# A decoder step's feed-forward down product: two of three token slices computed as seven rounds of half products

## The chip, the core and the metric

The kernel runs as one program on one core of a Trainium2 chip. The metric is the device time of one execution in microseconds (us). The engines named here: PE (TensorE, the matrix engine; PEld is its weight load), DVE (VectorE), ACT (ScalarE), POOL (GpSimd) and SP (SyncE, which only issues transfers). Each engine works through its own queue in order and waits for others by semaphores. Matrix products read SBUF and write PSUM; large arrays lie in HBM and move by DMA.

## What is computed

One step of a two-layer decoder (an mLSTM layer, then a forgetting-attention layer) for a prompt of 1024 tokens with 16 meta tokens and for 8 x 8 sample tokens, together 1104 tokens, model width 1024. Each layer ends with a feed-forward part, and that is what matters here:

```python
D_FF = -(-8 * D_MODEL // (3 * 256)) * 256          # 2816

def swiglu(xn, w_gu, w_d):
    gu = xn @ w_gu
    return (jax.nn.silu(gu[..., :D_FF]) * gu[..., D_FF:]) @ w_d
...
        h = h + swiglu(rmsnorm(h, prm['norm_ffn'][l]), prm['w_gate_up'][l], prm['w_down'][l])
```

The last product, the hidden activations (1104 x 2816) by `w_down` (2816 x 1024), is called the down product.

## The kernel before

All products are made in pairs of rounded float32 (`fp32r`): an operand is split into a high part (cast on ACT) and a rest (subtraction on DVE; `split`, L330 to L332), and a product is three matmuls, high by high, high by rest, rest by high (`mm3`, L267 to L271). The tokens are cut into three slices of 368 (`SL`, t = 0, 1, 2). Activations stand with their features on the 128 partitions, so a hidden vector is 22 blocks of 128 rows (`NF`).

`ffn` (L1465) runs once a layer, with three parts.

*Gate/up* (L1654 to L1805). The gate and up products of hidden blocks 2 to 21 already work on combinations of slices and weights: a `Unit` makes 20 products of 6 matmuls for two blocks of rows and three slices, even units the gate, odd units the up side; DVE and ACT combine the PSUM banks into six results (`s1`, `c15`, `s2`, `e`, `t4`, `v2`, each 128x368). `out` (L1530) applies silu to an even unit's results and multiplies an odd unit's with them; the products are the hidden activations, stored to HBM (`hT`) by SP, six stores every second unit. POOL makes the weight sums that a unit needs (`PairWeights.sums`, L102 to L111), two units ahead, from weights that SP loads (L77). The first two blocks of rows are made directly (`direct`, L1654).

*The down loop* (L1821 to L1856). `seq` lists 66 units (t, z, c): slice t, half z of the 1024 outputs, c one of 11 pairs of hidden blocks. A unit takes one weight block of 256 x 512 and one activation block of 256 x 368 and makes 4 groups of 6 matmuls, one for each of 4 PSUM banks; 11 units accumulate, and at the last unit of such a run DVE adds each bank to the residual `H[t]` (L1834; the addition is L1491). Two units ahead of their use, `w_split` and `h_split` split the raw blocks; weights are loaded by SP (`w_load`, L1638) into three raw buffers (two slots and `wr`), activations by POOL (`h_load`, L1621) into three buffers (`hr`). Activations of a slice are loaded and split in its half z = 0 and kept for z = 1. Split weights rotate through four places, so a split waits until PE has left the unit four back.

*Beside the loop.* After a bank is added, `each` squares the row block on ACT and sums the squares on POOL (`add_sq`, L393 to L405). When a slice is done, `ends` starts a generator of which one step runs in each unit: in layer 0 the normalisation of the slice (`norm_x`, L407 to L441; storing it to HBM first, L616), in layer 1 the final normalisation, transposes and stores (`final`, L1873). The residuals are reloaded from HBM during the loop (L1851, at units 2, 16 and 38 in the program).

Order: inside the loop the orders of PE, DVE and ACT are those of the program (`manual_schedule`); POOL and SP are ordered by the planner that builds the kernel, which goes by when its own model finds an instruction ready, with the program's order as priority.

## Time and profile before

| what | value |
|---|---|
| time, median of 3 runs | 2844.2 us (2840.56 to 2845.89) |
| the profiled execution's own time | 2841.83 us |
| span of its trace | 2840.1 us |
| granted TensorE clock, mean | 0.996 |
| HBM read, written | 299.5 MB, 96.8 MB |
| POOL's activation loads for the loop (L1621), all | 60 of 368 KB, and 8 more into the slices' own space |
| SP's weight loads for the loop | 88 into the two slots, 42 into `wr`, 2 into other space |

The down loops of layer 0 and layer 1 stand at 998.9 to about 1267 us and about 2557 to 2829 us. In a row of a table by stretch, each engine's busy us are followed by its instructions in brackets. In a row of groups, after the bar: busy us of the group, mean ns of one instruction, idle us of the engine just before, and what ended that idle time. A timeline row gives the start, the length, engine, line, operation, tiles, and in brackets the idle time before it. A tile's name is followed by others where buffers are shared: `vA` (layer 0) and `Ht` (layer 1) hold residuals, raw weights and intermediate results.

### The profile page before, as it was taken

The numbers are of one execution on the slowest core, as the hardware profiler recorded it, in microseconds if no ns is written. First come the engines' busy times: TensorE is split into PE (matmuls) and PEld (weight loads), VectorE is DVE, ScalarE is ACT, GpSimd is POOL, SyncE is SP. The second block draws the span as 40 slices with busy tenths as digits, with TensorE's granted clock in tenths as the row PEclk, the third lists the DMA queues.
The fourth block names the chain that finished last, engine by engine and source line by source line (L and its number), as shares of the span: only waits on it lengthen the run. The fifth ranks groups of instructions, "written<-read, shape, count | busy, mean of one in ns | idle before, by whom it ended". The sixth has DMA issues, their size and how long they took to land. (4 is left out here: it accounts for less than half of the span.)

```text
span 2840.1 us, 54146 instructions
## 1 busy us (share of the span) xinstructions
PE 2773.6 (98%) x20630; PEld 2651.7 (93%) x20630; DVE 1743.6 (61%) x3606; ACT 1318.1 (46%) x2636; POOL 1085.0 (38%) x1582
## 2 busy tenths in 40 slices
PE   8999998999999999999999999999999999999999
PEld 7997988999999999999999888777999999999998
DVE  6144566687787755553466543777478777775553
ACT  6122464444444434443345444877344454443432
POOL 3042333066656411117572202555307666631210
PEclk9999999999999999999999999999999999999999
DMA  7156664122222275644453676442413222236653
GB/s 218 29 139 166 164 182 156 53 89 77 82 85 79 94 267 194 207 156 142 132 174 120 238 289 221 135 171 88 159 50 91 78 78 90 77 109 243 214 191 106
DMA packets 313974, 399.81 MB, mean 141 GB/s; under 512 B 28966, under 2 KB 235794, under 8 KB 312690
## 3 DMA queue, kind: packets, MB, share of 16 engines
q1 hardware_dynamic: 277282, 277.66, 30.8%
q0 software_dynamic: 35680, 118.12, 12.9%
q8 instruction: 162, 2.65, 0.4%
q14 instruction: 98, 0.80, 0.1%
q10 hardware_dynamic: 752, 0.57, 0.1%
HBM read 299.50 MB, written 96.77 MB: 140 GB/s over the span
## 5 line engine op out<-in xcount | busy, mean ns | idle before, releaser
L332 DVE TENSOR_TENSOR slot<-slot,slot 128x1024 fp32r<-128x1024 f32 (+3 forms) x263 | 252.6, 962 | 117.2 <-ACT slot L331 111.8
L331 ACT CAST slot<-slot 128x1024 fp32r<-128x1024 f32 (+3 forms) x263 | 206.5, 787 | 227.9 <-PE dps L270 95.9
L1515 PE MATMUL m<-x0h,slot 128*128 128x368 f32 x640 | 178.3, 329 | 0.0
L1515 PE MATMUL m<-x1h,slot 128*128 128x368 f32 x640 | 174.1, 331 | 2.7 <-DVE ns L1492 0.9
L1621 POOL DMA_DIRECT2D hr<-hT x60 | 32.5, 541 | 271.9 <-DVE T_2l L332 68.1
L111 POOL TENSOR_TENSOR slot<-vA 128x256 f32<-128x256 f32 x80 | 75.4, 952 | 149.8 <-DMA vA<-in_w_gate_up 77.6
L111 POOL TENSOR_TENSOR slot<-Ht 128x256 f32<-128x256 f32 x80 | 75.1, 949 | 150.3 <-DMA Ht<-in_w_gate_up 78.6
L1515 PE MATMUL m<-x2h,slot 128*128 128x368 f32 x480 | 132.3, 330 | 0.0
L332 DVE TENSOR_TENSOR slot<-Ht,slot 128x256 fp32r<-128x256 f32 (+3 forms) x101 | 88.1, 874 | 56.3 <-ACT slot L331 56.3
L332 DVE TENSOR_TENSOR slot<-vA,slot 128x256 fp32r<-128x256 f32 (+3 forms) x101 | 88.1, 874 | 55.4 <-ACT slot L331 55.4
L1515 PEld LDWEIGHTS m<-x1h,slot 128*128 128x128 f32 x640 | 115.6, 188 | 4.6 <-DVE vA L1491 1.5
L1515 PEld LDWEIGHTS m<-x0h,slot 128*128 128x128 f32 x640 | 116.1, 188 | 0.0
L405 POOL TENSOR_TENSOR ns<-ns,nq 128x368 f32<-128x368 f32 x50 | 56.6, 1133 | 142.5 <-ACT nq L403 136.5
L1515 PE MATMUL m<-x1l,slot 128*128 128x368 f32 x320 | 105.6, 330 | 0.0
L1515 PE MATMUL m<-x0l,slot 128*128 128x368 f32 x320 | 105.5, 330 | 0.0
L2641 ACT ACTIVATE s<-s,nb 128x272 f32<-128x272 f32 (+7 forms) x126 | 98.8, 786 | 0.0
L2676 ACT COPY th<-tp 128x768 f32<-128x768 f32 (+1 forms) x80 | 73.6, 921 | 47.4 <-PE tp L2668 25.8
L1515 PE MATMUL m<-T_2h,slot 128*128 128x368 f32 x320 | 93.8, 334 | 0.4 <-ACT vA L1521 0.4
L1515 PE MATMUL m<-T_4h,slot 128*128 128x368 f32 x320 | 93.7, 334 | 0.0
L326 DVE SCALAR_TENSOR_TENSOR slot<-slot,gain,slot 128x256 fp32r<-128x256 f32 (+2 forms) x152 | 63.7, 466 | 43.5 <-ACT slot L325 41.1
L332 DVE TENSOR_TENSOR slot<-wr,slot 128x1024 fp32r<-128x1024 f32 x42 | 53.5, 1274 | 60.0 <-ACT slot L331 60.0
L1515 PEld LDWEIGHTS m<-x2h,slot 128*128 128x128 f32 x480 | 86.9, 188 | 0.0
(867 smaller groups left out, 10362.3 us busy)
## 6 DMA issues: line engine op xcount, KB each, us to landing
slot<-in_w_down SPq DMA_DIRECT2D x88, 512.0 KB, 4.6
hr<-hT POOLq DMA_DIRECT2D x60, 368.0 KB, 5.4
wr<-in_w_down SPq DMA_DIRECT2D x42, 512.0 KB, 3.8
wraw<-in_w_in_a SPq DMA_DIRECT2D x40, 512.0 KB, 4.2
vA<-in_w_gate_up SPq DMA_DIRECT2D x40, 512.0 KB, 4.1
Ht<-in_w_gate_up SPq DMA_DIRECT2D x40, 512.0 KB, 4.2
kp<-in_cache_k SPq DMA_DIRECT2D x32, 512.0 KB, 5.9
vp<-in_cache_v SPq DMA_DIRECT2D x32, 512.0 KB, 8.4
```

Source lines behind the costliest of these rows:

```text
L111: self.net.nc.gpsimd.tensor_tensor(out=o, in0=a, in1=b, op=op)
L326: nc.vector.scalar_tensor_tensor(out=lo[:, k], in0=raw[:, k], scalar=gk, in1=hi[:, k].bitcast(F32), op0=ALU.mult, op1=ALU.subtract)
L331: self.nc.scalar.copy(hi, src)
L332: self.nc.vector.tensor_tensor(out=lo, in0=src, in1=hi.bitcast(F32), op=ALU.subtract)
L405: (nc.vector if x >= late else nc.gpsimd).tensor_tensor(out=s, in0=s, in1=sq, op=ALU.add)
L1515: nc.tensor.matmul(u.b[b][:, :SL], w[p][:, k], x[q][:, k], start=new and k == i == 0, stop=k == 1 and i == 2, skip_group_check=True)
L1621: nc.gpsimd.dma_start(hraw[j], hT[t][:, 2 * c : 2 * c + 2])
L2641: nc.scalar.activation(ss[z, u], ss[z, u], AF.Exp, bias=nb[:, z : z + 1], accum_out=sm[:, u, z : z + 1])
L2676: nc.scalar.copy(th.rearrange("p x z (u h q) -> p h (x z u) q", h=2, q=64)[:, :, :n], pt[:, :, :n])
```

## The change

For hidden blocks 2 to 21, the down products of slices 1 and 2 are no longer made as four sets of products (two slices, two output halves) but as seven. Slices 1 and 2 with the even and odd hidden blocks are a 2 x 2 matrix of activations A11, A12 (slice 1, even and odd) and A21, A22 (slice 2); the weights with even and odd hidden blocks and the two output halves are a 2 x 2 matrix too. `ROUNDS` lists the seven products in their order, each as (number, weight block to load, which results it is added to, with sign): 5 (A11 + A12), 1 (A11 + A22), 3 (A11), 7 (A12 - A22), 4 (A22), 2 (A21 + A22), 6 (A21 - A11). Each round is 5 units of 256 hidden rows.

- The loop has 61 units: 22 for slice 0 as before, 4 for the first pair of hidden blocks (slices 1 and 2, both halves, each a run of its own), 35 for the rounds.
- The five sums of activations are made in gate/up by POOL (`combine`), once an odd unit, from its results, over the buffers of those results; five sums and the two plain blocks that rounds 3 and 4 need go to HBM (`hA`), with slice 0's two: nine stores every second unit.
- Of the weights, two of the four blocks are loaded once and kept (the odd block of half 1 in round 5, in the space of slice 1's activations; the even block of half 0 in round 1, in the space of gate/up's `T` tiles). Rounds 5 and 2 use a kept block as it is. Rounds 1, 3, 7, 4 and 6 need a sum or difference of two blocks, made on POOL (`w_sum`, 128x1024) before the split: round 1 from both kept blocks, the others from a newly loaded and a kept one.
- Every round's activations are loaded and split: 48 loads a layer in place of 34; weight blocks are split 59 times in place of 66, loaded 54 times in place of 66.
- A round's banks are added to up to two results (12 additions of four tiles over the seven rounds, and 4 more for the first pair of hidden blocks, in place of 4 in all).
- Slice 1 is done after round 4 and slice 2 after round 6; in the last two rounds two steps of the generator run a unit, and three of the pending squares. The splits stand ahead of a unit's matmuls in the program, behind them before.
- The residuals' reload stands at units 2, 14 and 18, and the final output's buffers are others.

```diff
+ROUNDS = ((5, None, ((1, 1, 1), (1, 0, -1))), (1, None, ((1, 0, 1), (2, 1, 1))), (3, (0, 1), ((1, 1, 1), (2, 1, 1))),
+          (7, (1, 0), ((1, 0, 1),)), (4, (1, 0), ((1, 0, 1), (2, 0, 1))), (2, None, ((2, 0, 1), (2, 1, -1))),
+          (6, (0, 1), ((2, 1, 1),)))
...
-    hT = [self.dram.tile([P, NF, SL], F32, name=f"hT{l}_{t}") for t in range(3)]
+    hT = [self.dram.tile([P, NF if t == 0 else 2, SL], F32, name=f"hT{l}_{t}") for t in range(3)]
+    hA = {r: self.dram.tile([P, NF // 2 - 1, SL], F32, name=f"hA{l}_{r}") for r in range(1, 8)}
...
                     tt(out=o, in0=o, in1=keep[t, i], op=ALU.mult)
-                    nc.sync.dma_start(hT[t][:, u.f + i], o)
+                    if t == 0:
+                        nc.sync.dma_start(hT[0][:, u.f + i], o)
+                    elif (t, i) in ((1, 0), (2, 1)):
+                        u.send(3 if t == 1 else 4, c)
                 else:
                     nc.scalar.activation(o, o, AF.Silu)
                     keep[t, i] = o
+
+            def send(u, r, c):
+                nc.sync.dma_start(hA[r][:, u.f // 2 - 1], u.c[c])
+
+            def combine(u):
+
+                pool = lambda o, i, j, op: nc.gpsimd.tensor_tensor(out=u.c[o], in0=u.c[i], in1=u.c[j], op=op)
+                for r, o, i, j, op in ((7, "v2", "s1", "t4", ALU.subtract), (5, "s1", "s1", "s2", ALU.add),
+                                       (1, "c15", "s2", "t4", ALU.add), (2, "t4", "t4", "e", ALU.add),
+                                       (6, "e", "e", "s2", ALU.subtract)):
+                    pool(o, i, j, op)
+                    u.send(r, o)
...
-        seq = [(t, z, c) for t in range(3) for z in range(2)
-               for c in ((*range(1, NC), 0) if (t, z) == (2, 1) else range(NC))]
-
-        hseq = [i for i, (t, z, c) in enumerate(seq) if z == 0 or (t, c) == (2, 0)]
-        hraw, hpart, wraw, wpart = {}, {}, {}, {}
+        NR = (NC - 1) // 2
+        ws = [("p", 0, c, z) for z in range(2) for c in range(NC)] + [("p", 1, 0, z) for z in range(2)]
+        ws += [("r", x, q, None) for x in range(len(ROUNDS)) for q in range(NR)]
+        hs = [(0, c) for c in range(NC)] + [(1, 0), (2, 0)] + [("r", x, q) for x in range(len(ROUNDS)) for q in range(NR)]
+
+        seq = [(j, j % NC, 0, j // NC, j % NC == 0, j % NC == NC - 1) for j in range(2 * NC)]
+        seq += [(2 * NC + z, NC + t - 1, t, z, True, True) for z in range(2) for t in (1, 2)]
+        seq += [(2 * NC + 2 + i, NC + 2 + i, None, i // NR, i % NR == 0, i % NR == NR - 1) for i in range(len(ROUNDS) * NR)]
+        wneed, hneed = ([max(e[k] for e in seq[: i + 1]) for i in range(len(seq))] for k in (0, 1))
+        flow = [j for j, w in enumerate(ws) if w[0] == "p" or ROUNDS[w[1]][0] not in (5, 2)]
...
+                if hs[j][0] == "r":
+                    _, x, q = hs[j]
+                    src = hA[ROUNDS[x][0]][:, 2 * q : 2 * q + 2]
...
+                y = (x0 + x1 + a)[j] if j < NC else x2[(j - NC) % 4]
+                hpart[j] = tuple(p[:, : 2 * SL].rearrange("p (k n) -> p k n", k=2) for p in y)
+                self.split(hraw.pop(j), *hpart[j])
...
+        halves = wd.rearrange("(c h p) n -> p h c n", h=2, p=P)
+
+        def own(h, q):
+
+            if h:
+                if q % 3 == 0:
+                    kept["x", q // 3] = self.xp.tile([P, KT * SLA], F32, name=self.uid("wx"), tag="x1" + "hl"[q // 3])
+                return view(kept["x", q // 3][:, q % 3 * KT * P : q % 3 * KT * P + KT * P])
+            return view(fp.tile([P, 4 * SL], F32, name=self.uid("wt"), tag="T%d%s" % ((2, 1, 4)[q // 2], "hl"[q % 2])))
...
+                if i in flow:
+                    k = flow.index(i)
+                    if k < 3:
+                        wraw[i] = view((self.slots[0], self.slots[1], flat[1])[k])
+                    else:
+                        wraw[i] = view((self.slots[0], self.slots[1], wr)[(k if kind == "p" else k + 2) % 3])
+                if kind == "p":
+                    nc.sync.dma_start(wraw[i], wd[2 * q * P : 2 * q * P + 2 * P, 512 * z : 512 * z + 512].rearrange(
+                        "(k p) n -> p k n", p=P))
+                    return
+                r, b, _ = ROUNDS[x]
+                part = lambda h, z: halves[:, h, 1 + 2 * q : 3 + 2 * q, 512 * z : 512 * z + 512]
+                if r in (5, 1):
+                    h = 1 if r == 5 else 0
+                    kept[h, q] = own(h, q)
+                    nc.sync.dma_start(kept[h, q], part(h, h))
+                if r in (5, 2):
+                    wraw[i] = kept[1 if r == 5 else 0, q]
+                if b:
+                    nc.sync.dma_start(wraw[i], part(*b))
+
+        def w_sum(i):
+            if i < len(ws) and ws[i][0] == "r":
+                _, x, q, _ = ws[i]
+                r, b, _ = ROUNDS[x]
+                if i in flow:
+                    nc.gpsimd.tensor_tensor(out=wraw[i], in0=wraw[i] if b else kept[0, q],
+                                            in1=kept[0 if r in (4, 6) else 1, q], op=ALU.subtract if r in (3, 4) else ALU.add)
 
         def w_split(i):
-            if i < len(seq):
-                wpart[i] = tuple(view(self.slots[y]) for y in (2 + i % 4, LOW[i % 4]))
+            if i < len(ws):
+                p = (i + max(0, min(3, (i - 2 * NC + 3) // 5))) % 4
...
+                    if g == 2 and v.odd:
+                        v.combine()
...
+            u.combine()
...
+            for i, (wi, hi, t, z, lead, last) in enumerate(seq):
+                n = SL
+                k, todo = min(i + 2, len(seq) - 1), None
+                while wj < wneed[k]:
+                    wj += 1
+                    w_split(wj)
+                    todo = wj
+                while hj < hneed[k]:
+                    hj += 1
+                    h_split(hj)
+                    h_load(hj + 3)
+                if todo:
+                    w_sum(todo + 1)
+                if len(seq) - 4 < i < len(seq) - 1 and after:
+                    early(i - len(seq) + 3)
+                wh, wl = wpart[wi]
+                ah, al = hpart[hi]
+                to = ((t, z, 1),) if t is not None else ROUNDS[z][2]
...
-                        add(H[t][:, 4 * z + m], H[t][:, 4 * z + m], o)
-                        pend.append(lambda t=t, m=4 * z + m: each(t, m))
+                        for tt_, zz, sign in to:
+                            y = H[tt_][:, 4 * zz + m]
+                            (add if sign > 0 else sub)(y, y, o)
+                        if (t == 0 or (t is None and ROUNDS[z][0] in (3, 4, 2, 6))):
+                            tq, zq = (0, z) if t == 0 else {3: (1, 1), 4: (1, 0), 2: (2, 0), 6: (2, 1)}[ROUNDS[z][0]]
+                            done.append(tq)
+                            x = done.count(tq) - 1
+                            pend.append(lambda t=tq, m=4 * zq + m, x=x: each(t, m, x))
+                            if x == KT - 1 and tq < 2:
+                                pend.append(lambda t=tq: ends(t))
...
-                if last and z and t < 2:
-                    pend.append(lambda t=t: ends(t))
-                w_split(i + 2)
...
-                if i + 2 in hseq:
-                    h_split(hj)
-                    h_load(hj + 3)
-                    hj += 1
-                w_load(i + 5)
-                if i in (2, 16, 38):
-                    y = (2, 16, 38).index(i)
+                if todo:
+                    w_load(todo + 3)
+                if i in (2, 14, 18):
+                    y = (2, 14, 18).index(i)
                     nc.gpsimd.dma_start(H[y], self.hD[:, :, TS[y][0] : TS[y][1]])
-                next(steps, None)
+                late = t is None and z > 4
+                for _ in range(0 if late and last else 2 if late else 1):
+                    next(steps, None)
                 if not last:
-                    for _ in range(2):
+                    for _ in range(3 if late else 2):
                         if pend:
                             pend.pop(0)()
+            for _ in steps:
...
-    out = flat[(2, 0, 1)[t]]
+    out = flat[t - 1] if t else self.xp.tile([P, KT * SLA], F32, name="outs", tag="x0h")
```

47 lines of the change are left out of this document (19 added, 28 removed).

## The prediction

> **What bounds the kernel now.** I read the page's first lines, then the table of busy time by stretch (laid over the down loop), then the groups by line with shapes kept apart, then timelines of single engines.
>
> ```profile
> span 2840.1 us, 54146 instructions
> PE 2773.6 (98%) x20630; PEld 2651.7 (93%) x20630; DVE 1743.6 (61%) x3606; ACT 1318.1 (46%) x2636; POOL 1085.0 (38%) x1582
> ```
>
> TensorE is the bound of nearly the whole span, so the question is whether the down loop is one of its saturated stages. Its six stretches of layer 0, then one of layer 1 (us; busy us and instructions of PE, PEld, DVE, ACT, POOL; clock, DMA share, GB/s):
>
> ```profile
> 998.90:1043.00 44.10, 44.10 (x264) 44.10 (x263) 22.99 (x25) 16.63 (x20) 8.35 (x13) 1.00 0.90 320
> 1043.00:1087.40 44.40, 44.40 (x267) 44.40 (x266) 17.78 (x17) 15.57 (x19) 5.65 (x8) 1.00 0.43 139
> 1087.40:1131.70 44.30, 44.30 (x264) 44.06 (x263) 29.52 (x36) 20.13 (x26) 7.56 (x13) 1.00 0.74 250
> 1131.70:1176.00 44.30, 44.30 (x266) 44.30 (x265) 20.92 (x26) 18.72 (x25) 4.86 (x8) 1.00 0.43 139
> 1176.00:1220.00 44.00, 44.00 (x262) 43.76 (x261) 29.23 (x36) 18.96 (x25) 7.19 (x11) 1.00 0.67 235
> 1220.00:1265.00 45.00, 45.00 (x270) 45.00 (x269) 25.46 (x38) 19.96 (x33) 4.10 (x6) 1.00 0.43 136
> ...
> 2691.00:2735.00 44.00, 44.00 (x264) 44.00 (x264) 16.83 (x16) 15.34 (x18) 5.25 (x4) 1.00 0.42 141
> ```
>
> The reader is to see three things. PE is busy through every stretch, at a granted clock of 1.00: 264 matmuls, that is 11 units of 24, take 44.1 us, so a unit is 4.02 us and a matmul 0.167. VectorE has room: 17 to 30 us of 44. The stretches with new activations (first, third, fifth) move 235 to 320 GB/s, the others 139, and PE is full in both. So a matmul taken out of this loop shortens the span by 0.167 us, as long as the others keep two units ahead.
>
> **The change part by part.** What it removes: the old loop has 66 units a layer (3 slices x 2 halves x 11). The new one has 22 for slice 0, 4 for the first pair of rows of slices 1 and 2, and 7 rounds of 5: 61. Five units fewer a layer are 5 x 24 x 0.167 = 20.1 us, 40.2 us for both layers. This is the only gain; everything else is work put beside PE.
>
> ```profile
> L332 DVE TENSOR_TENSOR slot<-wr,slot 128x1024 fp32r<-128x1024 f32 x42 | 53.5, 1274 | 60.0 <-ACT slot L331 60.0
> L332 DVE TENSOR_TENSOR x2l<-hr,x2h 128x736 fp32r<-128x736 f32 x16 | 14.7, 916 | 1.0 <-ACT x2h L331 1.0
> L1491 DVE TENSOR_TENSOR Ht<-Ht,dps 128x368 f32<-128x368 f32 x24 | 12.9, 538 | 51.4 <-PE dps L271 51.4
> ...
> L331 ACT CAST slot<-wr 128x1024 fp32r<-128x1024 f32 x42 | 44.1, 1049 | 84.2 <-PE dps L270 53.6 <-DMA wr<-in_w_down 30.7
> ...
> L331 ACT CAST x2h<-hr 128x736 fp32r<-128x736 f32 x16 | 12.9, 806 | 3.0 <-DMA hr<-hT 2.7
> ...
> L111 POOL TENSOR_TENSOR vA<-vA 128x512 f32<-128x512 f32 x40 | 59.2, 1480 | 15.3 <-DVE wl0l L332 15.3
> L405 POOL TENSOR_TENSOR ns<-ns,nq 128x368 f32<-128x368 f32 x50 | 56.6, 1133 | 142.5 <-ACT nq L403 136.5 <-ACT x1h L331 5.0 <-issue 0.2
> L1621 POOL DMA_DIRECT2D hr<-hT x60 | 32.5, 541 | 271.9 <-DVE T_2l L332 68.1 <-DVE T_4l L332 60.0 <-DVE x1l L332 48.9
> L2071 POOL TENSOR_TENSOR raw<-raw,gk 128x768 f32<-128x768 f32 x12 | 22.7, 1891 | 38.1 <-PE btp L2049 38.1
> ```
>
> ScalarE: a round unit splits one weight block (1.05) and one activation block (0.81), 1.9 us of 4.02: hidden. VectorE: 1.23 (the undisturbed time of the split, below) + 0.92 = 2.15 us a unit, and the round ends add 12 half slices of 4 tiles, 48 x 0.54 = 26 us over 35 units, 0.74 each; 2.9 of 4.02, hidden if nothing slows it. At a round's end up to 8 additions (4.3 us) must free four banks; each bank needs 1.1 us and PE returns to it 3 us after leaving it, so about 4 us of VectorE backlog are harmless there.
>
> GpSimd: 25 of the 35 round units need a weight sum of 128x1024, a shape that no row has. From below, the 768 row scaled by 4/3 gives 2.5 us; from above, two 512 sums give 3.0. I take 2.6, near the longest row. With the load issue (0.54) that is 3.1 of 4.02 us. It lengthens the ring of three raw buffers: load, sum 2.6, cast 1.05, rest 1.23, and the next load.
>
> ```profile
> slot<-in_w_down SPq DMA_DIRECT2D x88, 512.0 KB, 4.6
> hr<-hT POOLq DMA_DIRECT2D x60, 368.0 KB, 5.4
> ```
>
> 4.6 + 2.6 + 1.05 + 1.23 = 9.5 us, against 12.1 for three units: it holds with 2.6 us to spare. Two rounds take a kept block and load no sum at all; round 1 adds two kept blocks. SP's queue issues at most one weight load and no store in a round unit, fewer in total than before (54 loads against 66); the 14 additional activation loads are GpSimd's. The highest traffic, a weight and an activation block per unit, is that of the 235 GB/s stretch, where PE was full.
>
> Here the covers touch: a split reads both operands from SBUF, and so does the weight sum. The timelines of GpSimd and VectorE at 1042 show what that does:
>
> ```profile
> 1042.20 0.98 POOL L405 TENSOR_TENSOR ns<-ns,nq 128x368 f32<-128x368 f32 x1 [8.18 <-ACT nq L403]
> 1044.54 2.96 POOL L405 TENSOR_TENSOR ns<-ns,nq 128x368 f32<-128x368 f32 x2 [1.37 <-ACT nq L403]
> ```
>
> ```profile
> 1043.52 3.14 DVE L332 TENSOR_TENSOR slot<-slot,slot 128x1024 fp32r<-128x1024 f32 x2
> 1046.58 2.00 DVE L332 TENSOR_TENSOR slot<-wr,slot 128x1024 fp32r<-128x1024 f32 x1
> 1049.38 1.23 DVE L332 TENSOR_TENSOR slot<-slot,slot 128x1024 fp32r<-128x1024 f32 x1 [0.80 <-ACT slot L331]
> ```
>
> Alone the sum took 0.98 and the split 1.23. Together two sums took 2.96 instead of 1.96, and three splits 5.06 instead of 3.69. So 1.96 us of GpSimd arithmetic cost VectorE 1.37, 0.70 us for each. If all of a unit's 2.6 us fell on splits VectorE would lose 1.8, if none 0. Splits cover somewhat over half of a unit, so I take two thirds, 1.2 us: 4.1 us a sum unit on average, against 4.02. VectorE goes from half idle to just full in the sum rounds.
>
> What shows is where something else comes on top. In layer 0 the normalisation of slice 0 runs one step a unit after its last unit, on units 29 to 40, so over rounds 1 and 3. Its size: the third and fourth stretch hold 29.52 + 20.92 = 50.4 us of VectorE, of which 22 weight splits, 11 activation splits and 8 additions are 41.5; 9 us remain. Ten units of rounds 1 and 3 then need 2.15 + 0.86 (16 additions) + 0.75 + 1.2 = 5.0 against 4.02, 10 us too much. The splits run two units ahead and the banks allow 4 us, so I let 4 us reach PE; bounds 0 and 10. In layer 1 the output of slice 0 stands there in place of it, one burst in a loop with the same margins: 1 us, bounds 0 and 5. The doubled steps of slice 1 in the last two rounds meet one round with sums: within these bounds.
>
> In gate/up five GpSimd sums of 128x368 (about 1.1 each, 5.7 us) and three stores more come on every second unit. Timelines of GpSimd, VectorE and ScalarE, two units around 724:
>
> ```profile
> 722.73 1.53 POOL L111 TENSOR_TENSOR vA<-vA 128x512 f32<-128x512 f32 x1 [1.59 <-DVE wl0l L332]
> 728.80 1.44 POOL L111 TENSOR_TENSOR slot<-vA 128x256 f32<-128x256 f32 x2 [4.55 <-DMA vA<-in_w_gate_up]
> ```
>
> ```profile
> 724.46 0.53 DVE L1534 TENSOR_TENSOR vA<-vA,vA 128x368 f32<-128x368 f32 x1
> ```
>
> ```profile
> 734.38 0.45 ACT L1521 COPY vA<-m 128x368 f32<-128x368 f32 x1
> ```
>
> The last operand is done at 725.0, where GpSimd waits 4.6 us for a load. The five sums fill that gap and push the next by a microsecond or two. The new wait is that of the copy at 734.4, which overwrites a buffer still being stored: behind it on ScalarE stand the next unit's copies and weight casts. The sum it needs ends near 727 and its store 2 us later, 5 us ahead of need. I take 0.5 us for both layers.
>
> Sum, against the profiled execution (2841.8): -40.2 + 4 + 1 + 0.5 = -34.7, so 2807. The median of the runs lies 2.4 above that execution: **2809**.
>
> **Rivals.**
> *The pair serializes.* If a split and a weight sum can't overlap at all, a sum unit needs 2.6 + 2.15 = 4.75 us of the two, 0.73 over PE's 4.02; over 25 units 18 us a layer, less some 6 of lead, and the normalisation's 4 and 1: 29 us of 40 are lost, 2833 on the scale of the median. For it: both slow each other in every overlap. Against it: strictly in turn the stretch from 1043.52 would have lasted 3.69 + 1.96 = 5.65 us, and it took 5.06. The Trainium skill (SBUF — State Buffer, Who interferes with whom) calls the shared pair of ports an exclusive lock, so that the later instruction blocks wholly; by that rule this rival would be the forecast, and the row of 5.06 us speaks for something milder.
>
> *GpSimd's order, the case on the slower side.* Sum and activation load share GpSimd's queue, and the load waits for VectorE's split. If the sum of the next block stands behind that load, each waits for the other in a circle: sum 2.6, cast 1.05, split 1.23, activation split 0.92, issue 0.54, 6.3 us a unit and no overlap. Over 25 sum units 58 us a layer, less 8 of lead: +100, 2909. It decides as soon as the circle passes 4.02 us. For it: the loads' 271.9 us of waiting on VectorE. Against it: GpSimd's order isn't the program's.
>
> ```profile
> 1006.93 0.55 POOL L1621 DMA_DIRECT2D hr<-hT x1 [5.01 <-DVE x1l L332]
> 1007.47 0.90 POOL L1851 DMA_DIRECT2D vA<-hD  x1
> 1013.33 0.55 POOL L1621 DMA_DIRECT2D hr<-hT  x1 [4.97 <-DVE x1l L332]
> 1017.59 0.54 POOL L1621 DMA_DIRECT2D hr<-hT  x1 [3.71 <-DVE x1l L332]
> 1018.18 0.90 POOL L1851 DMA_DIRECT2D vA<-hD  x1
> ```
>
> The slice loads of units 16 and 38 (L1851) left within the first five units, each when it was ready; a sum ready two units early would likewise go ahead.
>
> *Combining late.* If GpSimd makes the five sums behind the next weight sums (after 737), the copy at 734.4 waits until about 741, 7 us in each of ten unit pairs, mostly on the path: 140 us in all, 2949. Only an order against readiness does this.
>
> *It doesn't do what it says* would be a unit count not falling to 61; the loops leave no room for that.
>
> **How the numbers follow.** Forecast 2809 (from 2802 with no loss to 2822 with both upper bounds and a little of the ring): 0.64. Serialized pair 2833 (2822 to 2845): 0.22. GpSimd's order 2909: 0.09. Combining late 2949: 0.03. Something unseen, mostly slower: 0.02. A measurement of this kernel tells 0.2%, 5.7 us, from no change. Faster takes the forecast and three quarters of the serialized case: 0.81. Same takes the rest of that: 0.06. Slower 0.13. The range from 2801 to 2838 leaves out the two orders and the end of the serialized case.
>
> **What would show it.** Right: PE busy in all stretches of a loop of some 246 us (before 266), weight sums of 2.5 to 3.5 us, splits between 1.23 and 2.0. The rivals: PE gaps at the starts of rounds 3 and 7 with VectorE solidly busy (pair); weight sums directly behind activation loads and units of over 6 us (order); ScalarE waiting for a store in gate/up (combining). Wrong altogether: a split of above 2 us throughout, or weight loads landing in over 7 us.

## The result, and the profile after

The changed kernel takes 2916.7 us (median of 4 runs, 2916.07 to 2919.66), the kernel before on the same chip 2843.05 us. The ratio is 1.0261, with a 95% interval of 1.0243 to 1.0279: the change makes the kernel 2.6% slower, where 1.2% faster was forecast and the range ended at 2838.

The first lines of the page of the changed kernel (busy time, share and instructions of each engine):

```profile
span 2917.9 us, 54140 instructions
...
PE 2767.5 (95%) x20390; PEld 2631.4 (90%) x20390; DVE 1938.5 (66%) x3716; ACT 1322.9 (45%) x2650; POOL 1343.4 (46%) x1760
```

The 240 matmuls are gone (20630 before, 20390 now), yet PE is busy nearly as long as before (2767.5 us against 2773.6), and its share fell from 98% to 95%. Busy time of VectorE grew by 195 us and that of GpSimd by 258. What PE waits for is in the view of waits over the whole span (us in total, times, longest):

```profile
PE m L1521 <- DVE ns L1498: 26.4, 19, 2.0
PE dps L274 <- ACT ns L405: 12.6, 3, 8.7
PE dps L274 <- DVE vA L1497: 11.5, 2, 8.3
PE nps L418 <- DVE ns L410: 8.7, 1, 8.7
```

Three of the four wait for VectorE, and none was in the trace of before at that size (0.9, none, none and 0.3 us there). The second names a square on ScalarE (`add_sq`); the longest of its waits ends at 1215.15 us, within 0.2 us of the additions on VectorE that free the bank (two of 0.46 from 1214.03), so it may be a wait for them as well. The down loop of layer 0, in the view by stretch (us; busy time and instructions of PE, PEld, DVE, ACT, POOL; clock, DMA share, GB/s):

```profile
1070.00:1110.00 40.00, 40.00 (x240) 40.00 (x239) 17.67 (x17) 14.63 (x17) 5.14 (x7) 1.00 0.61 204
1110.00:1150.00 40.00, 40.00 (x239) 39.76 (x238) 24.90 (x34) 14.20 (x19) 18.80 (x14) 1.00 0.46 152
1150.00:1190.00 40.00, 31.10 (x168) 30.55 (x167) 33.37 (x40) 13.23 (x18) 18.93 (x13) 0.87 0.46 133
1190.00:1230.00 40.00, 30.59 (x171) 30.02 (x170) 33.75 (x33) 17.05 (x24) 24.85 (x20) 0.87 0.56 171
1230.00:1270.00 40.00, 36.74 (x203) 36.46 (x203) 39.01 (x32) 17.77 (x23) 28.39 (x20) 0.91 0.54 171
```

Up to the end of round 5 (no sums) PE makes 240 matmuls in 40 us, as before. In the rounds with sums it makes 168 to 203. VectorE is busy 33 to 34 of 40 us in the first two of these stretches and 39 in the third: in the first two, where PE gets least done, VectorE isn't full. The prediction has no place for that.

The stages show where the time went. Their lengths are read from PE's timeline: gate/up from its first matmul to the first of the down loop, the loop from its first to its last matmul, the end of layer 0 from there to the first matmul of the next layer's output projection. "Due" is the loop of before less 20.1 us.

| us | span | gate/up 0 | loop 0 | from loop 0 to next layer | gate/up 1 | loop 1 |
|---|---|---|---|---|---|---|
| before | 2840.1 | 409.0 | 267.1 | 735.5 | 408.8 | 271.9 |
| due | 2799.9 | 409.0 | 247.0 | 735.5 | 408.8 | 251.8 |
| after | 2917.9 | 432.9 | 284.9 | 742.3 | 433.6 | 271.6 |
| lost against due | 118.0 | 23.9 | 37.9 | 6.8 | 24.8 | 19.8 |

The remaining 4.8 us (118.0 less the five) lie mostly ahead of gate/up of layer 0, where the change does nothing and the start of that stage scatters from 587.7 to 594.5 us between the kernels of this study. So there are three places: gate/up lost 48.7 us, the loops 57.7, the end of layer 0 6.8.

Three cuts of timelines say how. First GpSimd and VectorE of the changed kernel in gate/up, where four of the five new sums (L1554) stand together (the fifth comes some 7 us earlier):

```profile
776.41 1.15 POOL L1554 TENSOR_TENSOR vA<-vA 128x368 f32<-128x368 f32 x1
777.52 1.26 POOL L1554 TENSOR_TENSOR vA<-vA,nr 128x368 f32<-128x368 f32 x1
778.86 1.05 POOL L1554 TENSOR_TENSOR nr<-nr,vA 128x368 f32<-128x368 f32 x1
779.99 1.15 POOL L1554 TENSOR_TENSOR vA<-vA 128x368 f32<-128x368 f32 x1
```

```profile
777.88 1.18 DVE L337 TENSOR_TENSOR slot<-slot,slot 128x256 fp32r<-128x256 f32 x1
778.99 1.32 DVE L1497 TENSOR_TENSOR ns<-ns,fs 128x368 f32<-128x368 f32 x1
780.23 1.46 DVE L337 TENSOR_TENSOR slot<-slot,slot 128x512 fp32r<-128x512 f32 x1
781.61 0.53 DVE L1498 TENSOR_TENSOR ns<-m,ns 128x368 f32<-128x368 f32 x1
```

GpSimd works without a gap for 4.7 us, and in that time every VectorE operation takes over a microsecond, down to the smallest. From 781.1 to 782.3 GpSimd is idle, and an addition of 128x368, here with an operand in PSUM, takes 0.53. In the trace of before the split of 128x256 from one slot to another takes 418 ns on average (the groups of VectorE from 700 to 780 us, shapes kept apart):

```profile
L332 DVE TENSOR_TENSOR slot<-slot,slot 128x256 fp32r<-128x256 f32 x4 | 1.7, 418 | 0.0
```

VectorE has no idle time in these rows, and the addition that frees PE's bank (781.61) stands behind them; PE waits 1.37 us for it. All of PE's waits in gate/up are for additions and copies out of its banks and none for a weight block, so it isn't that GpSimd's own weight sums come late.

Second, VectorE and GpSimd of the changed kernel at the end of round 1, where the blocks of round 3 are split:

```profile
1169.94 0.53 DVE L430 TENSOR_TENSOR npy<-vA,nr 128x368 f32<-128x368 f32 x1
1171.96 1.23 DVE L337 TENSOR_TENSOR slot<-slot,slot 128x1024 fp32r<-128x1024 f32 x1 [1.49 <-ACT slot L336]
1173.10 3.09 DVE L337 TENSOR_TENSOR x2l<-hr,x2h 128x736 fp32r<-128x736 f32 x1
1176.12 0.53 DVE L433 TENSOR_TENSOR x0l<-npy,x0h 128x368 fp32r<-128x368 f32 x1
1176.57 0.53 DVE L430 TENSOR_TENSOR npy<-vA,nr 128x368 f32<-128x368 f32 x1
...
1181.27 3.65 DVE L1497 TENSOR_TENSOR vA<-vA,dps 128x368 f32<-128x368 f32 x8
```

```profile
1172.42 2.99 POOL L1702 TENSOR_TENSOR slot<-slot,wx 128x1024 f32<-128x1024 f32 x1 [2.02 <-DMA slot<-in_w_down]
1176.49 0.55 POOL L1652 DMA_DIRECT2D hr<-hA  x1 [1.08 <-DVE x2l L337]
1177.05 2.37 POOL L1702 TENSOR_TENSOR slot<-slot,wx 128x1024 f32<-128x1024 f32 x1
```

The sum waits 0.6 us for the split that stands ahead of it (2.99 instead of 2.37), and then the split behind takes 3.09 us instead of 0.92: it stands still for 2.17. And beside it VectorE idles 1.49 us for ScalarE, every unit. That wait is no work of the new sums; it was there before. Third, VectorE and then ScalarE of the kernel **before**, in its own loop, where the normalisation of slice 0 runs (its lines are 5 or 6 lower):

```profile
1114.06 0.55 DVE L425 TENSOR_TENSOR npy<-vA,nr 128x368 f32<-128x368 f32 x1
1116.09 1.23 DVE L332 TENSOR_TENSOR slot<-slot,slot 128x1024 fp32r<-128x1024 f32 x1 [1.48 <-ACT slot L331]
1117.23 0.92 DVE L332 TENSOR_TENSOR x1l<-hr,x1h 128x736 fp32r<-128x736 f32 x1
1118.07 0.54 DVE L428 TENSOR_TENSOR x0l<-npy,x0h 128x368 fp32r<-128x368 f32 x1
1118.52 0.54 DVE L425 TENSOR_TENSOR npy<-vA,nr 128x368 f32<-128x368 f32 x1
```

```profile
1114.64 0.47 ACT L426 CAST x0h<-npy 128x368 fp32r<-128x368 f32 x1 [4.89 <-DVE npy L425]
1115.01 1.05 ACT L331 CAST slot<-slot 128x1024 fp32r<-128x1024 f32 x1
```

It is a ring through two engines whose orders are fixed by the program. VectorE multiplies a row for the normalisation; ScalarE copies it, and only behind that copy stands its cast of the next weight block; VectorE's rest waits for the cast, and the next product stands behind the two rests. Once around takes 4.46 us (1114.06 to 1118.52), where PE needs 4.02 for a unit. Before, the lead of two units bore 0.4 us for eight units. In the changed kernel the same ring goes around in 6.63 us (1169.94 to 1176.57), which is 4.46 and the 2.17 that the split stood still. Over the eight products from 1162.65 to 1209.32 one turn takes 6.67 us on average (one of the seven has eight additions in it).

PE meets this lateness at the starts of rounds, where it needs its banks back. It starts the last matmul of round 1 at 1173.81; VectorE, behind with the ring, begins the eight additions only at 1181.27 (above). All waits of PE of over 1.1 us in this loop stand at such a start; the two longest, ahead of rounds 3 and 7:

```profile
1182.39 0.64 PE L274 MATMUL dps<-x2h,slot 128*128 128x368 f32 x1 [8.25 <-DVE vA L1497]
...
1215.15 0.65 PE L274 MATMUL dps<-x2h,slot 128*128 128x368 f32 x1 [8.66 <-ACT ns L405]
```

### The profile page after: what moved, and what is told of

Its sections match the earlier page's. It is cut to its first block, busy times and chain, and to the rows that moved or that the text cites. A ratio compares the mean times of both kernels' runs of the same rounds, so it can differ in the third digit from the quotient of the medians.

```text
span 2917.9 us, 54140 instructions
## 1 busy us (share of the span) xinstructions
PE 2767.5 (95%) x20390; PEld 2631.4 (90%) x20390; DVE 1938.5 (66%) x3716; ACT 1322.9 (45%) x2650; POOL 1343.4 (46%) x1760
## 5 line engine op out<-in xcount | busy, mean ns | idle before, releaser
L337 DVE TENSOR_TENSOR slot<-slot,slot 128x256 fp32r<-128x256 f32 (+1 forms) x239 | 271.8, 1138 | 93.6 <-ACT slot L336 89.8
L336 ACT CAST slot<-slot 128x256 fp32r<-128x256 f32 (+1 forms) x239 | 181.7, 762 | 205.4 <-PE m L1521 71.3
L274 PE MATMUL dps<-x2h,slot 128*128 128x368 f32 x624 | 215.0, 345 | 35.4 <-ACT ns L405 12.6
L275 PE MATMUL dps<-x2l,slot 128*128 128x368 f32 x624 | 212.3, 340 | 1.8 <-DVE x2l L337 1.8
L276 PE MATMUL dps<-x2h,slot 128*128 128x368 f32 x624 | 211.8, 339 | 0.0
L1521 PE MATMUL m<-x1h,slot 128*128 128x368 f32 x640 | 180.3, 336 | 28.1 <-DVE ns L1498 26.4
L274 PEld LDWEIGHTS dps<-x2h,slot 128*128 128x128 f32 x624 | 122.7, 197 | 38.5 <-issue 16.8
L337 DVE TENSOR_TENSOR slot<-Ht,slot 128x256 fp32r<-128x256 f32 (+3 forms) x101 | 94.5, 937 | 50.7 <-ACT slot L336 30.7
L275 PEld LDWEIGHTS dps<-x2l,slot 128*128 128x128 f32 x624 | 122.8, 197 | 2.5 <-DVE x2l L337 2.3
L276 PEld LDWEIGHTS dps<-x2h,slot 128*128 128x128 f32 x624 | 122.4, 196 | 0.0
L1652 POOL DMA_DIRECT2D hr<-hA x70 | 38.3, 547 | 164.1 <-DVE x2l L337 154.3
L337 DVE TENSOR_TENSOR x2l<-hr,x2h 128x736 fp32r<-128x736 f32 x74 | 108.8, 1473 | 0.0
```

What stands on the lines that cost most here:

```text
L274: mm(ps, sh, mh, start=first, stop=False)
L275: mm(ps, sh, ml, start=False, stop=False)
L276: mm(ps, sl, mh, start=False, stop=last)
L336: self.nc.scalar.copy(hi, src)
L337: self.nc.vector.tensor_tensor(out=lo, in0=src, in1=hi.bitcast(F32), op=ALU.subtract)
L1521: nc.tensor.matmul(u.b[b][:, :SL], w[p][:, k], x[q][:, k], start=new and k == i == 0, stop=k == 1 and i == 2, skip_group_check=True)
```

## The experiments

The theories at the start: **A**, VectorE stands still while GpSimd sums (in gate/up and in the loops; called the lock below); **B**, sum and load form a circle in GpSimd's queue; **C**, the new stores of gate/up are the cost there; **D**, something in the loop apart from the sums. E, R and V came up on the way. Stage lengths are in us; where only one time is given, the kernel before took 2846.49 beside e1 to e4 and 2842.13 (median) beside e5 to e7. e1 to e4, e6 and e7 are single runs.

**e1: the loads of activations on SyncE's queue** in place of GpSimd's.

```
-                nc.gpsimd.dma_start(hraw[j], src)
+                nc.sync.dma_start(hraw[j], src)
```

> The changed kernel with the loop's activation loads issued by SP in place of GpSimd, nothing else. Its trace shows 24 us lost in each gate/up and 58 us of the 40 us gain eaten in the two down loops (285 and 272 us where 247 were due). Theory A (a GpSimd sum and a VectorE split of two SBUF operands exclude each other): the sums stay where they are, so the loops stay within 10 us of 285 and 272, total 2905 to 2925. Rival B (the circle on GpSimd's queue: the sum of the next block stands behind a load that waits for VectorE's split): the loops fall to some 250 to 260 each, total 2880 or less.

2918.43; loops 288.7 and 277.3. B falls: without a load in GpSimd's queue nothing is faster, and the ring takes 6.62 us as in the changed kernel (products at 1167.98 and 1174.60 in its trace). PE now waits for casts of activation blocks too, 2.8 and 7.1 us in the two loops; that is less than the 25 to 35 and 12 to 22 us that B expected to gain.

**e2: the weight sums of the rounds on VectorE**, in the same place of the order.

```
-                    nc.gpsimd.tensor_tensor(out=wraw[i], in0=wraw[i] if b else kept[0, q],
+                    nc.vector.tensor_tensor(out=wraw[i], in0=wraw[i] if b else kept[0, q],
```

> The weight sums of the loop made by VectorE (about 1.2 us each) in place of GpSimd; the sums of activations in gate/up stay on GpSimd. Theory A and rival B both let the loops fall, A to some 262 (layer 0) and 252 us (layer 1), VectorE then holding 4.1 us of a 4.02 us unit, total about 2875; gate/up stays at 433. Rival D (VectorE is simply over its time, whoever makes the sums: additions, normalisation, splits): the loops stay at or above 285 and 272, total 2915 or more.

2923.42; gate/up 433.7 and 432.1, loops 286.7 and 272.4. These are D's numbers; the fall of the loops that A (to 262 and 252) and B expected is missed. Neither A nor B alone explains the loops: with no sum left on GpSimd there, they stay as long. The sum of 1.22 us on VectorE stands in the ring too, in place of the 2.17 lost.

**e3: gate/up without the five sums**, the stores kept.

```
-                    pool(o, i, j, op)
```

> The five GpSimd sums a unit pair of gate/up left out; the nine stores stay, storing the plain results, so rounds 5, 1, 7, 2 and 6 work on unsummed activations. Theory A: both gate/up parts return from 433 to about 410 us, total about 2870, the loops unchanged. Rival C (the three more stores, and the waits for buffers that are still being stored): gate/up stays within 5 us of 433, total 2910 or more.

2862.16; gate/up 408.4 and 408.8, as before the change; loops 284.5 and 270.0. The whole loss in gate/up (23.9 and 24.8) goes with the sums on GpSimd. C falls: the stores cost nothing that can be seen.

**e4: the sums of gate/up and of the rounds on VectorE** (the edit of e2, and the same for gate/up).

```
-                pool = lambda o, i, j, op: nc.gpsimd.tensor_tensor(out=u.c[o], in0=u.c[i], in1=u.c[j], op=op)
+                pool = lambda o, i, j, op: nc.vector.tensor_tensor(out=u.c[o], in0=u.c[i], in1=u.c[j], op=op)
```

> Both kinds of sums on VectorE, nothing of the change on GpSimd but the loads. Theory A: the loops as with the weight sums alone on VectorE (262 and 252), gate/up between 410 and 425, since VectorE takes 2.7 us more a unit pair without any exclusion: total 2830 to 2865. Rival C or D: 2900 or more.

2874.44; gate/up 411.1 and 411.4, loops 286.1 and 274.2. The same five sums that cost 24 us a layer on GpSimd cost 2 to 3 on VectorE (beside e3). The loops don't move: A's 262 and 252, and its 2830 to 2865, are missed again. VectorE's timeline of e4 in a round without normalisation shows a second ring:

```profile
1203.50 1.23 DVE L337 TENSOR_TENSOR slot<-slot,slot 128x1024 fp32r<-128x1024 f32 x1 [1.18 <-ACT slot L336]
1204.64 0.92 DVE L337 TENSOR_TENSOR x2l<-hr,x2h 128x736 fp32r<-128x736 f32 x1
1205.48 1.22 DVE L1702 TENSOR_TENSOR wr<-wr,wt 128x1024 f32<-128x1024 f32 x1
1207.87 1.23 DVE L337 TENSOR_TENSOR slot<-wr,slot 128x1024 fp32r<-128x1024 f32 x1 [1.17 <-ACT slot L336]
```

The sum of the next block stands behind the rests of this one, ScalarE casts only what is summed, and VectorE waits 1.17 us for that cast: 4.37 us a unit, above PE's 4.02. This is theory **E**: the place of the sum.

**e5: e4 with the sum of the next block ahead of the splits of this one.**

```
                 while wj < wneed[k]:
                     wj += 1
+                    w_sum(wj + 1)
                     w_split(wj)
...
-                if todo:
-                    w_sum(todo + 1)
```

> Both kinds of sums on VectorE as in e4, and the sum of the next weight block ahead of the split of this one in the program, in place of behind it. Theory E (a ring through two queues whose orders are written out: VectorE's sum or normalisation product, ScalarE's cast, VectorE's rest, then VectorE's next sum; in e4's trace 4.38 us a sum unit and 5.58 with a normalisation step, VectorE idle 1.2 to 1.5 us in each): VectorE's work without the idle time is some 3.7 us a unit, under PE's 4.02, so the loops fall from 286 and 274 to about 255 and 250, total 2810 to 2825. Rival D (VectorE has too much work, whatever its order): the loops stay within 8 us of 286 and 274, total 2865 or more.

2848.97, ratio 1.0031 (1.0020 to 1.0043); loops 267.2 and 261.6. The place of the sum was worth 18.9 and 12.6 us. The expected 2810 to 2825 isn't reached, so E is a part of it; D as the whole cause, by which no order would help, falls.

**e6: e4 without the weight sums.** The blocks go in unsummed.

```
-                if r in (5, 2):
+                if r in (5, 2, 1):
...
-                if todo:
-                    w_sum(todo + 1)
```

> Activation sums on VectorE, weight sums of the loop left out: rounds 1, 3, 7, 4 and 6 split their blocks unsummed. It shows what of the loops' loss is the sums'. Theory E: without sums only the normalisation's ring is left (4.45 us in the trace of before), 8 steps and 0.4 us each, within the lead: loops about 252 and 248. Rival D: additions and activation splits alone already fill VectorE, loops above 265 and 260.

2837.37; loops 263.4 and 256.7. With no sum at all the loop of layer 0 is still 16 us above due, so it isn't the sums alone. The ring of the normalisation, and bursts of eight additions behind two splits, are what is left in the order of VectorE; e8 to e10 try them.

**e7: e5 with the weight sums on GpSimd**, ahead of the splits.

```
-                    nc.vector.tensor_tensor(out=wraw[i], in0=wraw[i] if b else kept[0, q],
+                    nc.gpsimd.tensor_tensor(out=wraw[i], in0=wraw[i] if b else kept[0, q],
```

> Activation sums on VectorE, weight sums on GpSimd as in the change, but ahead of the split in the program as in e5. Where theory A (exclusion of GpSimd sum and VectorE split) is a cost of its own, the loops stay clearly above those of e5, 265 or more and 260 or more. Where only the place of the sum counts, they come within 5 us of e5's.

2875.26; loops 285.3 and 271.9, 18 and 10 more than e5. With e2 this is the reading of the loops: A and E are each enough to hold them at 285 and 272. Taking away the lock alone (e2) or moving the sum alone (e7) gains nothing; both together (e5) gain 28 us of the loops.

**e8: e5 with the ring opened.** The product stands first in a unit, the copy behind the two casts.

```
             y = pp.tile([P, 512], F32, name=self.uid("npy"), tag="n")[:, :n]
+            yield "front"
             nc.vector.tensor_tensor(out=y, in0=H[t][:, k], in1=r, op=ALU.mult)
-            nc.scalar.copy(xh[:, k], y)
             yield
+            nc.scalar.copy(xh[:, k], y)
             nc.vector.tensor_tensor(out=xl[:, k], in0=y, in1=xh[:, k].bitcast(F32), op=ALU.subtract)
...
+                if front and not (late and last):
+                    step()
```

> All sums on VectorE and ahead of the splits, as in e5, and now the normalisation of a slice is put into the round units in another order: the product of the next row is VectorE's first work of a unit, ahead of the split, and ScalarE copies it behind the unit's two casts instead of ahead of them. Nothing is computed differently. Theory R: what is left in e6, which has no sums at all and still takes 263 us for the loop of layer 0 where 247 are due, is a ring through VectorE and ScalarE (product, copy, cast, two rests, product: 4.45 us a unit with 1.48 us of it idle on VectorE) that stands above PE's 4.02. Opened, the loop of layer 0 falls from 267 us in e5 to 253 to 258, the wait of about 8.7 us of PE at the end of layer 0 shrinks, the loop of layer 1 stays at 262, and the kernel takes 2825 to 2833. Rival V (VectorE simply has too much work with the sums, additions and the normalisation together): the loop of layer 0 stays within 3 us of 267, and the kernel at 2845 to 2850.

2840.19, ratio 0.9992 (0.9981 to 1.0003); loops 263.8 and 261.2. Between R and V: the kernel lies below V's 2845 to 2850 and above R's 2825 to 2833. By the ratios it is 0.4% faster than e5. The trace shows 3 us of that in loop 0, but it is the trace of an execution of 2850.74 us, 10 above the median, so how the gain is spread over the stages isn't known.

**e9: e8 with the additions ahead of the splits**, the order of the kernel before (the whole block of the two `while` loops moves behind the unit's matmuls and additions).

```
-                while wj < wneed[k]:
...
-                    h_load(hj + 3)
                 wh, wl = wpart[wi]
...
+                while wj < wneed[ahead]:
...
+                    h_load(hj + 3)
                 if todo:
                     w_load(todo + 3)
```

> e8 with one more edit: the splits for the unit after next stand behind the additions of a round's end in VectorE's order, as in the kernel before, and not ahead of them. Theory B (the bursts of eight additions, 3.7 us, hold four banks up because two splits and a sum stand in front of them; PE waits for them 9 us in the loop of layer 0 of e5): PE's waits for the additions go, and the kernel gains another 5 to 10 us against e8. Rival L (then VectorE waits through the last unit of each round for PE's banks, and the split of the next unit comes too late): PE's waits for the rests of the splits appear at the start of each of seven rounds, 2 us or more each, and the kernel is 15 to 30 us slower than e8.

2839.43, ratio 0.9992 (0.9982 to 1.0001); loops 261.4 and 261.6. Neither B (here the bursts of additions) nor L: the kernel takes as long as e8, where B expected 5 to 10 us less and L 15 to 30 more. The waits for the additions shrank in loop 0, and waits for the rest of the activation split took their place, 6.6 us in five pieces. What both come from stands in the view by stretch of e9:

```profile
1152.00:1172.00 20.00, 17.98 (x105) 17.69 (x106) 20.00 (x29) 9.13 (x13) 2.15 (x4) 1.00 0.63 191
...
1192.00:1212.00 20.00, 19.50 (x117) 19.19 (x116) 20.00 (x22) 11.10 (x13) 4.68 (x8) 1.00 0.75 239
```

Now VectorE is full, 20.00 of 20, with the sums on it. Whatever is put first, something else is late.

**e10: e9 without the weight sums.**

```
-                if r in (5, 2):
+                if r in (5, 2, 1):
...
-                    w_sum(wj + 1)
```

> e9 without the weight sums of the seven rounds (the blocks go into the products unsummed; round 1 takes a kept block): the floor of the new loop, once the ring is opened and the additions stand ahead of the splits. Theory V: in e9 VectorE is the bound of the rounds with sums (20.0 us busy of 20 in 1152 to 1172 and 1192 to 1212), so without them both loops come near their due times of 247 and 252 us: 248 to 254 in layer 0, 252 to 257 in layer 1, and the kernel takes 2818 to 2828. Rival Q (something beside VectorE's work, such as late blocks from memory or the additions, holds the loops): layer 0 stays at 258 or above and the kernel at 2832 or above, no better than e6.

2825.01, ratio 0.9935 (0.9916 to 0.9955); loops 249.7 and 257.1. As V expects for layer 0, 2.7 us above due; layer 1 lies 5.3 above due and 0.1 above V's range. In these stretches of e10's rounds PE doesn't wait any more:

```profile
1120.00:1160.00 40.00, 40.00 (x238) 39.76 (x237) 35.00 (x50) 22.60 (x30) 4.83 (x9) 1.00 0.49 145
1160.00:1200.00 40.00, 40.00 (x240) 40.00 (x240) 30.30 (x39) 20.08 (x27) 10.10 (x14) 1.00 0.69 231
```

Beside e6 this shows that ring and additions together held loop 0 by 13.7 us (and loop 1 not at all: 256.7 and 257.1), and beside e9 that the sums cost 11.7 and 4.5 us even on VectorE. It also shows PE full at 231 GB/s with VectorE at 30 to 35 of 40 us: the new loop is sound as far as traffic and lead go.

**e11: e9 with slice 0's normalisation sooner** (squares and first steps in the units of the first pair, two steps a unit in round 5) and no steps of slice 1's in the last two units.

```
-                if front and not (late and last):
+                if front and i < len(seq) - 2:
...
-                left = 0 if late and last else 2 if late else 1
+                left = 0 if i > len(seq) - 3 else 2 if late or t is None and z == 0 else 1
...
-                if not last:
+                if not last or t in (1, 2):
```

> e9 with slice 0's normalisation begun in the units of the first pair and run at two steps a unit in round 5, which has no sums, and with no step of slice 1's normalisation in the last two units of the loop (they run behind the last additions). Nothing is computed differently. Theory V (VectorE is the bound where sums and the normalisation meet): the loop of layer 0 falls from 261 to 254 to 258 us and the wait of 8 us at the end of layer 0 by 2 to 4; the kernel takes 2830 to 2836, below the kernel before by more than 0.2%. Rival: the work only moves within rounds that are full anyway; the kernel stays within 3 us of e9's 2839.

2838.84, ratio 0.9980 (0.9969 to 0.9990); loops 263.8 and 260.2. The rival holds: the work moves within rounds that are full. The kernel is 0.2% below the kernel before, just at what can be told, and no other of the study that has all the sums is faster.

**e12: e9 with the weight sums on GpSimd**, ahead of the splits, the ring open (the edit of e7 on e9).

> e9 with the weight sums of the rounds back on GpSimd, still ahead of the splits; the sums of gate/up stay on VectorE. The ring is open, the additions stand first, and VectorE has the work of e10's rounds, 30 us of 40. Theory A (while GpSimd sums, VectorE's operations on SBUF stand still): a sum of 2.4 us costs VectorE as much as one of its own of 1.2 us and about 1.2 us more; the loops of both layers are longer than in e9 (261 and 262), 268 or more in layer 0, and the kernel takes 2850 to 2880. Rival F (the two engines overlap well enough once VectorE has room, the 0.70 us for each of the prediction): a sum costs VectorE 1.2 to 1.7 us, the loops stay within 3 us of e9's, and the kernel at 2835 to 2843.

2855.01, ratio 1.0043 (1.0024 to 1.0063); loops 268.9 and 270.9. A, by 7.5 and 9.3 us a loop. VectorE and GpSimd of e12 in round 3:

```profile
1165.52 5.82 DVE L337 TENSOR_TENSOR slot<-wr,slot 128x1024 fp32r<-128x1024 f32 x1 [0.70 <-ACT slot L336]
...
1177.72 3.66 DVE L1498 TENSOR_TENSOR vA<-vA,dps 128x368 f32<-128x368 f32 x8
```

```profile
1164.92 2.42 POOL L1703 TENSOR_TENSOR slot<-slot,wx 128x1024 f32<-128x1024 f32 x1
1167.28 0.55 POOL L1653 DMA_DIRECT2D hr<-hA  x1
1167.84 2.41 POOL L1703 TENSOR_TENSOR slot<-slot,wx 128x1024 f32<-128x1024 f32 x1
...
1178.76 2.42 POOL L1703 TENSOR_TENSOR slot<-slot,wx 128x1024 f32<-128x1024 f32 x1 [0.66 <-DMA slot<-in_w_down]
```

One split of 1.23 us took 5.82: it began 0.6 us into the first of two sums and ended 1.1 us after the second, 4.6 us lost. The second sum, begun 2.3 us after the split, went ahead of it undelayed (2.41 us); the half microsecond between the sums, in which GpSimd issued a load, didn't let the split through. The eight additions, with one operand in PSUM, took 3.66 us through the whole of the third sum, 0.46 each, and that sum took 2.42 like the others: neither noticed the other.

## Why the prediction was wrong

- **The saving, 40.2 us: right.** 240 matmuls are gone, and e10's loops are 17.4 and 14.8 us shorter than before where 20.1 were due in each. (A slip without weight: with no loss the prediction's sum gives 2804 on the scale of the median, not 2802.)
- **The size of a weight sum, 2.6 us (2.5 to 3.0): nearly right.** It takes 2.37 undisturbed (1177.05 above), a little under the lower bound, and 2.99 where it waits for a split.
- **"1.96 us of GpSimd arithmetic cost VectorE 1.37, 0.70 us for each": wrong as a price.** The row was read rightly, but on short operations. A sum of 0.98 us cost VectorE 0.69, about 0.3 us of it costing nothing; of a sum of 2.4 us only 0.1 to 0.2 us cost nothing, and 2.2 to 2.3 were lost (3.09 against 0.92; 5.82 against 1.23 under two sums). In the prediction's own sum that price makes a unit 4.5 us instead of 4.1 (an estimate: two thirds of 2.6 us at 0.92 for each, on 2.15 and 0.74). The rule of the Trainium skill that the prediction quotes (SBUF — State Buffer, Who interferes with whom) comes close to these rows. The rival built on it had only 2833, because it too went through the next step.
- **"VectorE goes from half idle to just full": the step that failed for the loops.** It compares a sum of busy times, 4.1 us, with PE's 4.02. But VectorE waits in its order: 1.48 us a unit for ScalarE in the normalisation's ring, visible in the trace of before and not looked for. What the lock takes is added to that ring, whether VectorE is full or not: 4.46 + 2.17 = 6.63 us. A second ring, through the place of the sum, took 4.37 us a unit in e4 without any lock; in layer 1, in units without a step of normalisation, the changed kernel's splits come 4.6 us apart (2820.13, 2824.71, 2829.34). So 57.7 us instead of 5, beyond every bound given.
- **"The five sums fill that gap", 0.5 us: wrong, 48.7 us.** It was the largest miss of a single term, and no rival had this cause. Only GpSimd's own idle time and the buffer's store were looked at. The gap on GpSimd was there: its next operation, at 782.27, still waits 1.13 us for its load. What VectorE does in the gap wasn't asked, though the view by stretch of **before** has it busy 32 of 40 us there (after it, the same stretch of time in the changed kernel, which is 13 us later in its work by then, as the same weight sums of GpSimd at 769.26 and 782.27 show; PE makes 15 matmuls fewer, and VectorE is busy no longer):

```profile
764.00:804.00 40.00, 40.00 (x241) 39.81 (x240) 31.92 (x50) 19.23 (x41) 24.87 (x25) 1.00 0.26 82
```

```profile
764.00:804.00 40.00, 38.05 (x226) 37.42 (x225) 31.80 (x46) 18.46 (x38) 27.91 (x29) 1.00 0.31 96
```

  e3 and e4 settle it: without the sums, or with them on VectorE, gate/up is back.
- **"The splits run two units ahead and the banks allow 4 us": wrong for the bursts.** Eight additions stand behind two splits in VectorE's order, and behind all by which the rings have made VectorE late. PE waited up to 8.3 us for one (after). The waits for additions come and go with the order (e8, e9), though e9 as a whole is no faster than e8.
- **The end of layer 0, 0 us: wrong, 6.8.** Slice 1 is complete only after the fifth of seven rounds, so its normalisation runs in the last two, ahead of the last additions, and PE waits 8.7 us for the sum of squares (0.3 before). The wait is 8.1 to 8.7 us in e5, e6, e8, e9, e10 and e12, and 6.6 in e11, the one that takes the steps out of the last two units. So, by e11, these steps are the smaller part. In the trace of after, splits of the next stage's weights also stand ahead of the last sum of squares on VectorE (six from 1319.04, 4.91 us; the sum begins at 1323.88); what they cost wasn't tried.
- **The rivals.** "GpSimd's order" has nearly the measured time, 2909, by another mechanism: e1 takes the load out of GpSimd's queue and nothing gets faster. Its signs are in the trace all the same: weight sums directly behind activation loads (1176.49 and 1177.05 above) and units of over 6 us. "The pair serializes" was the right mechanism with a price of 29 us. Its gaps of PE at the starts of rounds 3 and 7 came (8.25 and 8.66 us), but VectorE wasn't solidly busy there; the lock cost most of the 48.7 us of gate/up (44.0 came back in e4, with the sums on VectorE), for which that rival had nothing, and in the loops 28 us (e7 against e5). "Combining late" didn't happen.
- **What stays open.** The rings, the lock and the bursts aren't additive, so the 57.7 us of the loops can't be cut into shares that hold in another order. The last 5 us of e10's loop 1 weren't pursued, and most of the wait at the end of layer 0 wasn't explained. A kernel with the sums neither on GpSimd nor on VectorE wasn't tried.

## What to carry to other kernels

Before giving work to an engine with idle time, write down the ring: which instruction of which engine must end before the next unit's same instruction begins, with the waits that the trace shows already; a new piece inside the ring is paid in full, even on an engine that is busy 33 of 40 us. An elementwise operation on GpSimd is to be priced as nearly the same time taken from VectorE (2.2 to 2.3 us for 2.4), whenever VectorE works on two SBUF operands; here the same sums cost 24 us a layer on GpSimd and 2 to 3 on VectorE. Where two causes are each enough, undoing either one alone shows nothing (e2, e7), so undo both before dropping a theory.

## What the runs showed of the hardware

- The lock between GpSimd and VectorE depends on where VectorE's operands lie: 128x368 with both in SBUF took 1.32 us beside GpSimd's sums (778.99 above); eight of that size with one operand in PSUM ran through a sum at 0.46 each (e12). The Trainium skill says so on the same page (SBUF — State Buffer, Who interferes with whom: one SBUF input doesn't contend); the trace agrees, and it prices an order: additions out of PSUM can be put beside GpSimd's work, splits can't.
- PE's granted clock falls behind long waits of PE: it is 0.87 in 1150 to 1230 us of the changed kernel, with waits of 8.25 and 8.66 us, and 1.00 in e10's 1120 to 1200, without waits. In e9 it stays at 1.00 in 1132 to 1212, through waits of up to 1.8 us; but behind one of 2.35 us matmuls start 0.31 us apart for 3 us, and 0.17 apart again after that:

```profile
1256.05 0.68 PE L275 MATMUL dps<-x2l,slot 128*128 128x368 f32 x1 [2.35 <-DVE x2l L337]
1256.52 0.51 PE L276 MATMUL dps<-x2h,slot 128*128 128x368 f32 x1
...
1259.49 0.33 PE L274 MATMUL dps<-x2h,slot 128*128 128x368 f32 x1
1259.65 0.34 PE L275 MATMUL dps<-x2l,slot 128*128 128x368 f32 x1
```

  So this wait costs some 1.6 us more than its length (an estimate: 11 matmuls from 1256.05 to 1259.49, at 0.167 us 1.84). The length alone doesn't decide: behind a wait of 2.55 us in e6 (to 1152.68) the matmuls stay 0.17 apart. Over the span of the changed kernel PE's busy time fell by 6.1 us where 240 matmuls at 0.167 make 40.2, at a mean clock of 0.984 against 0.996; by this estimate 34 of the 118 us are slower matmuls, and the other 84 are idle time of PE. Whether the gaps alone set the clock wasn't separated.
